# One group of eight PSUM banks in place of groups of three and five, in a hybrid state-space layer

## The chip, the cores and the metric

The kernel runs on one core of a Trainium2 chip. The metric is the device time of one execution in microseconds (us), as the median of several executions. Engines are named as in the profile: PE is TensorE's matrix products and PEld its weight loads, DVE is VectorE, ACT is ScalarE, POOL is GpSimd, SP is the engine whose queue issues the DMAs.

## What is computed

One layer of a sequence model over 512 latent tokens and a context of 256 tokens, width 1024. A normalised input goes through one wide projection; its columns feed three token mixers (an SSD scan with 16 heads, an mLSTM with 4 heads, a gated linear attention, GLA, with 4 heads), each run forwards and backwards. Each mixer's output is projected, the three are merged with gates, and one projection and a SwiGLU network follow. Cut to its joints:

```
h = concat(norm(ctx) * (1 + csc1) + csh1, norm(x) * (1 + sc1) + sh1)
parts = split(h @ w_in)
y_ssd, y_ml, y_gla = scans, both directions, of parts
merged = sum over the three of sigmoid(gate) * (y @ w_b)
x = x + g1 * (merged @ w_out)
x = x + g2 * ((silu(h2 @ w_g) * (h2 @ w_u)) @ w_ffn_out)
out = norm(x)
```

## The kernel before, in words

Activations lie channel by token: 128 channels on the partitions, 512 latent tokens (or 256 of the context) along the free dimension. Each fp32 weight is split into a high and a low part (`split` in `fetch`, lines 217 to 221: ACT makes the high part on line 218, DVE or POOL the low part on line 220), and a dense product of 1024 channels is 24 matmuls into one PSUM bank: eight slices of channels by three (high by high, high by low, low by high), line 321 in `dense`. A product with tokens on the partitions is `tok`, line 359. Weight pieces come by DMA into a ring of slots (line 226); a slot is free again once a dense product has read it.

PSUM has eight banks of 128 by 512 fp32. Before the change they are in two groups. `acc_bank` (line 176) gives a bank to dense products, from a group of three. `bank` (line 179) gives one to all other products: the transposes, the scans' small products, the row sums. It has a group of five. Each call makes a new tile; the tile takes a bank of its group that has been released, and the first matmul into it waits until the last reader of the bank's former tile is done. Banks are given to tiles when the program is built, not while it runs. I take it in what follows that a group hands out the bank that it has got back first.

Two things set the order of the work. PE's order is that of the Python code (line 1657, `manual_schedule` for PE alone). `jobs` (line 248) takes the dense products one by one from a queue, and after each one `advance` (line 301) moves every open scan on by a step, so PE runs a dense product, then a few scan products, then the next dense product, always in that order. The other engines' and the DMA queue's order is settled when the program is built, from what is ready there.

Places that the prediction speaks of:
- GLA's `decay` (line 1011): per direction a product of 512 (line 1024) and one of 256 (line 1028), each into a bank of its own, read by DVE on lines 1025 and 1029. They read `aup` and `sm`, which were made much earlier.
- GLA's scan: `pre` (line 1104) makes scaled queries and keys on POOL (lines 1112 to 1120), ACT (1121) and DVE (1122); `products` (line 1125) multiplies them on PE (line 1132), and ACT (line 1134, the first) or DVE (line 1136, the others) takes the result from its bank into `A`. `turn` transposes (line 1164), ACT reads (line 1165). `step` is lines 1170 and 1171. `head_turn` transposes on line 993 and ACT reads on line 996; POOL multiplies by the gate on line 1204.
- The mLSTM's `turn` transposes keys (line 864). The SSD scan's output is read from its bank by DVE on line 792.
- `gates` (line 450): ACT reads a bank on line 519.
- `prepare` (line 1267) splits the finished mixer outputs for the branch products: ACT on line 364, DVE on line 365.
- The feed-forward products (line 1828) use one bank of the first group and two of the second per block of 128 channels; ACT and DVE read them on lines 1839 to 1852.

Of the kernel before, what the change touches and what calls it, by code (L numbers as in the profile page):

```python
# [9 lines left out]
F32 = mybir.dt.float32  # L10
# [81 lines left out]
class Slots:  # L92


    def __init__(self, net, need):
        self.net, self.own, self.out = net, {}, {}
        self.more(need)
# [44 lines left out]
class Net:  # L142
    def __init__(self, ctx, tc, a, out, dump):
        self.ctx, self.tc, self.nc, self.a, self.out, self.dump = ctx, tc, tc.nc, a, out, dump
        nc = tc.nc
        self.V, self.S, self.G, self.T = nc.vector, nc.scalar, nc.gpsimd, nc.tensor
        self.dma = nc.sync.dma_start
        pool = lambda name, bufs=1, **kw: ctx.enter_context(tc.tile_pool(name=name, bufs=bufs, **kw))
        self.kp = pool("keep")
        self.wp = pool("w")  # L150
        self.pd = pool("pd", space=bass.MemoryType.PSUM)
        self.ps = pool("ps", space=bass.MemoryType.PSUM)
        self.dp = pool("dr", space=bass.MemoryType.DRAM)

# [19 lines left out]
            yield  # L174

    def acc_bank(self):
        return self.pd.tile([128, 512], F32, name="acc", bufs=3)

    def bank(self):
        return self.ps.tile([128, 512], F32, name="bank", bufs=5)  # L180

    def source(self, key):
        a = self.a
# [1831 lines left out]
```

## Time and profile before

| | us |
|---|---|
| Median of three runs | 1473.01 (1469.53 to 1474.08) |
| The profiled execution's own time | 1467.97 |
| Its span, first to last instruction | 1466.2 |
| PE busy | 1372.4 (94%) |
| DVE busy | 927.8 (63%) |
| ACT busy | 664.2 (45%) |
| POOL busy | 364.5 (25%) |

How to read it: a matmul's row starts when it starts, and what it waited for stands behind it in brackets as "[idle before <-the engine, tile and line whose end released it]". The granted clock (PEclk) is TensorE's clock as a share of 2.4 GHz; it has two levels here, 1.00 (2.4 GHz) and 0.50 (1.2 GHz). A wait for several things is put down to the one that came last.

### The profile page before, as it was taken

To read this page: it belongs to the slowest core of one execution; us is meant where nothing else is said; L and a number is where in the kernel's file an instruction comes from. 1 tells how busy PE (TensorE), PEld (TensorE's weight loads), DVE (VectorE), ACT (ScalarE), POOL (GpSimd) and SP (SyncE) were. 2 spreads that over 40 slices of the span, in tenths; PEclk is the share of its full clock that TensorE was granted. 3 is DMA by queue.
4 is the path that set the end of the run, shared out by engine and by line. 5 is a ranking of instruction groups with operands and counts; after the bars stand their busy time and mean duration, and the time that the engine had idled before them with its cause. 6 is when DMAs were issued, how large, how long until landed. Compare 5 with 4: busy or idle time off the path is not lost. (4 is left out here: it accounts for less than half of the span.)

```text
span 1466.2 us, 22065 instructions
## 1 busy us (share of the span) xinstructions
PE 1372.4 (94%) x8136; PEld 1185.8 (81%) x8136; DVE 927.8 (63%) x1664; ACT 664.2 (45%) x1247; POOL 364.5 (25%) x330
## 2 busy tenths in 40 slices
PE   6998999999989999998997878999998999999997
PEld 4787789887778886886886866888778999998886
DVE  4557644968585567677675766434438988887332
ACT  5545464552244443334362553243346656566231
POOL 2115434124222123212324443134444000000011
PEclk9999999999999999999999998999998999999999
DMA  9323222333453224255546356757431333324331
GB/s 373 138 65 122 91 72 87 84 104 101 117 143 98 83 95 135 72 137 141 171 149 205 119 191 213 235 176 239 153 108 51 116 111 97 111 87 126 95 93 61
DMA packets 98411, 189.31 MB, mean 129 GB/s; under 512 B 10672, under 2 KB 19376, under 8 KB 97152
## 3 DMA queue, kind: packets, MB, share of 16 engines
q1 hardware_dynamic: 98304, 187.91, 41.3%
q8 instruction: 64, 1.05, 0.3%
q14 instruction: 43, 0.35, 0.1%
HBM read 166.73 MB, written 20.61 MB: 128 GB/s over the span
## 5 line engine op out<-in xcount | busy, mean ns | idle before, releaser
L321 PE MATMUL acc<-hlh,w 128*128 128x512 f32 (+1 forms) x1160 | 385.1, 400 | 6.1 <-ACT w L218 2.5
L218 ACT CAST w<-w 128x512 fp32r<-128x512 f32 (+1 forms) x302 | 182.8, 613 | 366.1 <-DMA w<-in_w_main_dram 162.0
L220 POOL TENSOR_TENSOR w<-w,w 128x512 fp32r<-128x512 f32 x125 | 173.8, 1390 | 540.0 <-ACT w L218 492.9
L321 PEld LDWEIGHTS acc<-hlh,w 128*128 128x128 f32 x1160 | 221.5, 191 | 57.9 <-ACT w L218 3.0
L220 DVE TENSOR_TENSOR w<-w,w 128x512 fp32r<-128x512 f32 x177 | 136.5, 774 | 203.9 <-ACT w L218 169.3
L321 PE MATMUL acc<-hll,w 128*128 128x512 f32 (+1 forms) x576 | 226.9, 394 | 0.9 <-POOL hll L1563 0.9
L321 PEld LDWEIGHTS acc<-hll,w 128*128 128x128 f32 x576 | 110.2, 191 | 23.6 <-POOL hll L1563 1.1
L1785 ACT CAST w<-w 128x512 fp32r<-128x512 f32 x140 | 85.0, 623 | 33.8 <-PE bank L1828 25.5
L321 PE MATMUL acc<-t,w 128*128 128x512 f32 x360 | 89.1, 401 | 9.9 <-ACT t L364 9.3
L1786 DVE TENSOR_TENSOR w<-w,w 128x512 fp32r<-128x512 f32 x140 | 94.5, 685 | 5.0 <-ACT w L1785 4.6
L359 PE MATMUL acc<-w,hlh 128*128 128x256 f32 x512 | 96.3, 290 | 0.2 <-POOL w L220 0.2
L1828 PE MATMUL acc<-th,w 128*128 128x256 f32 x480 | 95.5, 281 | 0.2 <-ACT fm L1839 0.2
L321 PEld LDWEIGHTS acc<-t,w 128*128 128x128 f32 x360 | 68.0, 190 | 26.7 <-ACT t L364 9.7
L1544 POOL TENSOR_TENSOR sq<-sq,sq 128x512 f32<-128x512 f32 x6 | 7.8, 1300 | 307.9 <-ACT sq L1542 307.9
L359 PEld LDWEIGHTS acc<-w,hlh 128*128 128x128 f32 x512 | 81.5, 194 | 3.4 <-issue 1.8
L439 DVE SCALAR_TENSOR_TENSOR cacc<-acc,c_scanc,cacc 128x510 f32<-128x510 f32 (+3 forms) x124 | 77.5, 631 | 6.7 <-ACT cacc L435 5.9
L1828 PEld LDWEIGHTS acc<-th,w 128*128 128x128 f32 x480 | 77.8, 188 | 0.5 <-ACT fm L1839 0.4
L321 PE MATMUL acc<-row,w 128*128 128x512 f32 (+1 forms) x360 | 76.3, 365 | 1.2 <-ACT row L367 0.7
L359 PE MATMUL acc<-w,hll 128*128 128x256 f32 x256 | 73.4, 287 | 0.0
L321 PEld LDWEIGHTS acc<-row,w 128*128 128x128 f32 x360 | 61.3, 189 | 13.6 <-ACT row L367 1.1
L1828 PE MATMUL acc<-tl,w 128*128 128x256 f32 x240 | 67.3, 281 | 0.0
L321 PE MATMUL acc<-hx,w 128*128 128x256 f32 (+1 forms) x432 | 63.7, 302 | 0.0
(454 smaller groups left out, 2902.4 us busy)
## 6 DMA issues: line engine op xcount, KB each, us to landing
w<-in_w_main_dram SPq DMA_DIRECT2D x180, 256.0 KB, 3.4
w<-in_w_ffs_dram SPq DMA_DIRECT2D x80, 256.0 KB, 2.7
t<-in_wmodT_dram SPq DMA_DIRECT2D x32, 512.0 KB, 3.9
w<-in_w_b_dram SPq DMA_DIRECT2D x48, 256.0 KB, 4.0
xk<-gd SPq DMA_DIRECT2D x40, 256.0 KB, 3.6
w<-in_w_ffo_dram SPq DMA_DIRECT2D x40, 256.0 KB, 2.6
wmod<-in_wmod_dram SPq DMA_DIRECT2D x8, 1024.0 KB, 11.0
row<-rows SPq DMA_DIRECT2D x16, 512.0 KB, 6.0
```

The costliest lines, as they stand in the source:

```text
L218: self.S.copy(h, w)
L220: self.LE[self.wcount % len(self.LE)].tensor_sub(l, w, h.bitcast(F32))
L321: self.T.matmul(dst, w[:, m0:m1], x[:, c0:c1], start=(k == 0 and j == 0), stop=(k == nk - 1 and j == 2))
L359: self.T.matmul(p, x[:, t0:t0 + 128], w, start=(k == 0 and j == 0), stop=(k == KT - 1 and j == 2))
L439: V.scalar_tensor_tensor(acc[:, o0:o1], p[:, o0 + d:o1 + d], w[:, cc, j:j + 1], acc[:, o0:o1], op0=OP.mult, op1=OP.add)
L1544: self.G.tensor_add(a, a, t)
L1785: S.copy(H, x)
L1786: le[p % 7].tensor_sub(L, x, H.bitcast(F32))
L1828: T.matmul(dst, x, y, start=(first and k == 0 and j == 0), stop=(k == 3 and j == 2), skip_group_check=True)
```

## The change

Both helpers now make a tile of the same group, `bank`, which has eight banks. The group of three is gone. Nothing else is touched: the same instructions are issued with the same operands, and only the numbers of the banks differ, and with them what a first matmul waits for.

```diff
         self.kp = pool("keep")
         self.wp = pool("w")
-        self.pd = pool("pd", space=bass.MemoryType.PSUM)
         self.ps = pool("ps", space=bass.MemoryType.PSUM)
...
     def acc_bank(self):
-        return self.pd.tile([128, 512], F32, name="acc", bufs=3)
+        return self.bank()
 
     def bank(self):
-        return self.ps.tile([128, 512], F32, name="bank", bufs=5)
+        return self.ps.tile([128, 512], F32, name="bank", bufs=8)
```

## Rows read from the trace of the kernel before

**Rows 1.** The page: the span, and each engine's busy time.
```profile
span 1466.2 us, 22065 instructions
...
PE 1372.4 (94%) x8136; PEld 1185.8 (81%) x8136; DVE 927.8 (63%) x1664; ACT 664.2 (45%) x1247; POOL 364.5 (25%) x330
```

**Rows 2.** Waits of PE, whole run: releaser, us in total, times, longest us.
```profile
PE acc L321 <- ACT t L364: 9.3, 1, 9.3
...
PE bank L1132 <- ACT xk L1165: 6.4, 1, 6.4
PE bank L1028 <- ACT xk L1134: 5.0, 1, 5.0
PE bank L1170 <- DVE xk L1136: 4.6, 2, 3.7
...
PE bank L864 <- DVE xk L792: 4.1, 1, 4.1
PE bank L1132 <- ACT t L519: 3.7, 1, 3.7
...
PE bank L1024 <- DVE t L1025: 1.5, 1, 1.5
...
PE bank L1024 <- DVE xk L1136: 1.2, 1, 1.2
...
PE acc L1828 <- ACT fm L1839: 0.2, 1, 0.2
```

**Rows 3.** Windows: stretch, length, busy us of the engines, PEclk, DMA share, GB/s.
```profile
133.30:136.70 3.40, 3.40 (x14) 3.21 (x15) 3.40 (x12) 2.44 (x8) 1.34 (x3) 0.50 0.25 80
404.60:432.90 28.30, 23.65 (x147) 20.82 (x148) 27.55 (x70) 11.53 (x22) 7.67 (x6) 0.88 0.55 150
423.90:430.20 6.30, 5.92 (x27) 5.52 (x28) 5.65 (x20) 2.95 (x6) 0.68 (x2) 0.50 0.54 164
432.90:457.60 24.70, 24.26 (x187) 22.16 (x185) 10.51 (x34) 11.16 (x21) 2.70 (x3) 1.00 0.30 84
795.80:798.90 3.10, 3.10 (x13) 3.01 (x14) 3.10 (x6) 1.76 (x4) 0.59 (x1) 0.50 0.49 184
822.80:826.20 3.40, 3.40 (x17) 3.31 (x16) 2.44 (x5) 2.20 (x4) 2.23 (x3) 0.50 0.54 201
870.60:873.90 3.30, 3.28 (x13) 3.18 (x14) 3.10 (x5) 2.51 (x5) 3.06 (x3) 0.50 0.00 0
1135.00:1330.00 195.00, 194.81 (x1638) 194.51 (x1637) 170.96 (x318) 120.66 (x244) 0.00 (x0) 1.00 0.35 106
```

**Rows 4.** Timeline of PE, 788 to 799 us: start, length, line, operands.
```profile
788.80 1.05 PE L1132 MATMUL bank<-row 128*128 128x128 f32 x8
789.69 0.49 PE L1164 MATMUL bank<-c_ident,row 128*128 128x128 f32 x3
789.94 0.48 PE L1024 MATMUL bank<-sm,aup 128*128 128x512 f32 x1
790.25 0.28 PE L1028 MATMUL bank<-sm,aup 128*128 128x256 f32 x1
790.37 0.40 PE L1024 MATMUL bank<-sm,aup 128*128 128x512 f32 x1
795.77 0.58 PE L1028 MATMUL bank<-sm,aup 128*128 128x256 f32 x1 [5.00 <-ACT xk L1134]
...
798.51 0.64 PE L321 MATMUL acc<-hlh,w 128*128 128x512 f32 x1
```

**Rows 5.** Timeline of ACT around 795 us.
```profile
794.61 0.62 ACT L218 CAST w<-w 128x512 fp32r<-128x512 f32 x1 [4.96 <-DMA w<-in_w_main_dram]
795.14 0.58 ACT L1134 COPY xk<-bank 128x512 f32<-128x512 f32 x1
```

**Rows 6.** Timelines of PE, POOL and ACT, 870 to 886 us.
```profile
885.76 0.79 PE L321 MATMUL acc<-t,w 128*128 128x512 f32 x1 [9.29 <-ACT t L364]
...
871.24 1.97 POOL L1204 TENSOR_TENSOR xk<-xk,xk 128x512 f32<-128x512 f32 x1 [0.24 <-ACT xk L996]
...
885.10 0.60 ACT L364 CAST t<-xk 128x512 fp32r<-128x512 f32 x1
```

## The prediction

> **What bounds the kernel now.** I read the page first. PE is busy 1372.4 of 1466.2 us [rows 1]: the kernel is bound by PE's row of products, run in a fixed order. A change that adds and removes no product can only alter the 93.8 us in which PE stands idle (1466.2 less 1372.4) and the stretches in which its clock is down.
>
> So the next view is the list of PE's waits [rows 2], read with one question: which of these waits is for data, and which for a bank? A wait is for a bank when the releaser reads a PSUM tile that the waiting product has no use for. Line 1028 multiplies `sm` by `aup`; its releaser, line 1134, copies a GLA product out of its bank. Nothing ties the two but the bank. Line 864 transposes mLSTM keys, and line 792 reads the SSD scan's output from its bank. By the same test lines 1165, 1136, 1025 and 519 are readers of other tiles' banks. Seven rows are of this kind: 6.4 + 5.0 + 4.6 + 4.1 + 3.7 + 1.5 + 1.2 = 26.5 us. Every one has `bank` as its tile, so each is a wait in the group of five. The largest wait of a dense product, 9.3 us behind line 364, is for data. For the group of three the list has a single row, 0.2 us behind line 1839. The banks that are short are those of the scans, while the dense products' three cost nothing.
>
> The third view is the granted clock behind these waits [rows 3]. After five of them it reads 0.50, the 1.2 GHz level: PE works 3.40 + 5.92 + 3.10 + 3.40 + 3.28 = 19.1 us there, and at 2.4 GHz that work would take half. The waits thus cost another 9.6 us, 36.1 us in all. That is the ceiling of what the change can give.
>
> **The change, part by part.** It issues no instruction more or less: matmuls, reads and DMAs are the same, on every queue. Its cost in work is nothing, and needs no cover. What it changes is when a product may start.
>
> Before, a scan product waits once five tiles of its group are unread, whatever the other three banks do. After, it waits only once eight tiles of any kind are unread. Eight unread tiles before the change would mean that both groups are full, when either kind of product would wait as well. If banks are handed out in the order in which they come back, the change therefore adds no wait of its own; it only takes some away. What remains to be worked out is how much of each wait goes and what is late next. With the clock's share, the five large places are:
>
> - 133 us, line 519's bank: 3.7 of wait and 3.40/2 = 1.7 of clock, 5.4 us.
> - 424 us, line 792's bank: 4.1 and 5.92/2 = 3.0, 7.1 us. Here DVE is the late one: it is busy 27.55 of 28.30 us up to 432.9 [rows 3], so PE gets ahead of it. But behind that it is busy 10.51 of 24.70 us only, waiting for others, and can catch up.
> - 795 us, line 1134's bank: five tiles are unread when PE comes to line 1028 again, namely lines 1132, 1164, 1024, 1028 and 1024 [rows 4]. ACT, which must read the first, has stood 4.96 us behind a weight cast that waited for its DMA [rows 5]. In one group of eight, line 1028, the next product and the next transpose take the sixth, seventh and eighth bank; the dense product after them would be the ninth, and stands until the first of the five is read at 795.7 us. It starts at 798.51 now. So 798.5 less 795.8, 2.7 us, is gained of 5.0 + 1.55: a dense product waits there for a scan's bank, which it never did before.
> - 822 us, line 1136's bank: 3.7 and 3.40/2, 5.4 us.
> - 870 us, line 1165's bank: 6.4 and 3.28/2 = 1.6, 8.0 us. I count nothing for it. The next thing PE needs is the split of line 364, which ACT ends at 885.7; PE stands 9.29 us for it already [rows 6]. ACT gets there behind a chain of POOL's work that begins after POOL's line 1204 at 871.24, itself released by ACT and not by PE. Earlier products at 864 would only make PE's wait at 885 longer.
>
> The small ones, 4.6 less 3.7 of line 1170, 1.2 and 1.5 of line 1024, are 3.6 us. Without the last place the sum is 5.4 + 7.1 + 2.7 + 5.4 + 3.6 = 24.2 us.
>
> Not all of that arrives at the end, since PE meets late data sooner. Places from 735 us on (1.5 + 2.7 + 5.4 = 9.6) all run into the wait at 885; ACT, POOL and the DMA queue come earlier to it only as far as they were held up by PE, and I keep a third, 3.2 us. Of the other 14.6 I keep two thirds, 9.7 us, since DVE, the busiest of the readers, has a third of its time free [rows 1] and mostly moves with PE. Bounds are none and all. Sum: 12.9, say **13 us**. From 900 us on there is next to nothing to gain: the only bank wait there is the one of 0.2 us.
>
> One cost has no row. PE's order is fixed, but the other queues' order is settled at building, and with other banks it may come out otherwise. The nearest row is ACT's 4.96 us behind one weight cast [rows 5]: one such meeting more or one fewer is 5 us either way. I take 0 and keep both ends.
>
> A rule speaks against the change. At full clock PE runs through the feed-forward products of 1135 to 1330 us, three banks to a block from both groups in turn, without a drop [rows 3]. The Trainium skill, TensorE: Matmul & The Clock Gate, "A second HAM failure mode: psum-queue depth-cycling", tells of a kernel whose turning through PSUM banks left small gaps between products, with the clock swinging between its levels. By it, eight banks in turn would bring more half-speed stretches; the trace speaks against that for this kernel.
>
> **The sum against the times.** The profiled execution took 1467.97 us, 5.0 below the median of 1473.01. 1468 less 13 is 1455; on the scale of the median, 1473 less 13 is **1460 us**.
>
> **Rivals.**
>
> *The waits only move (20%).* All that PE gains up to 870 us may be given back at 885, where it waits for the last mixer's output; and the DVE-bound stretch up to 432.9 may pass its lateness on to 457. For it: PE's 9.3 us is the largest wait after the start and lies right behind the bank waits. Against it: the chain to 885 begins with products that PE itself would deliver sooner. The time would be that of before, 1473, within 4 us. The same TensorE page, "HAM oscillation — how this bites in real kernels", reports a kernel in which double-buffered PSUM gave no further gain once its order of loops was right (126.6 against 125.5 us).
>
> *Slower (13%).* A dense product's bank may be one whose reader is late. Since banks are tied to tiles at building, a dense product may be given the bank of a scan tile that the builder thought read and that the chip reads late; before, a dense product could not meet one. The place is the GLA scans, four heads; the price is one wait like 5.0 or 6.4 us per head [rows 2], some 20 us with the gains above gone: up to 1493. It decides once two of four heads meet such a bank. Against it: the order of return must differ by three banks or more, as eight are in turn.
>
> *All of it (7%).* Every wait goes and the data come earlier with PE: 1473 less 36 is 1437.
>
> **How the numbers follow.** A measurement of this kernel tells a difference from none at about 0.3%, 4.4 us. My forecast, a gain between 5 and 28 us, has 60%. Faster by more than 0.3% is 60 + 7, 67%; within 0.3% 20%; slower 13%. The likeliest time is 1460. The range starts at 1473 less 28.1 (36.1 without the last place), 1445, and reaches past no change to 1475; below it lies the 7%, above it most of the 13%. The 5 us of the queues' order lie inside.
>
> **What would show it.** In PE's waits the rows behind 1134, 792, 519 and 1136 are gone or under 1 us, and the clock near 133, 424 and 822 us stays at 1.00; PE's busy time falls by the clock's share and its idle by more. Near 795 a dense product waits for line 1134. The wait of line 321 behind 364 grows from 9.3 towards 15 us. I am wrong if line 321 or 359 waits for lines 1134, 1136 or 1165 in several heads, or if the data waits grow by as much as the bank waits shrink.

## The result and the profile after

| | before | after |
|---|---|---|
| Median of runs on one chip, us | 1471.76 (1469.53 to 1474.08, 4 runs) | 1451.19 (1447.94 to 1455.69, 4 runs) |
| The profiled execution's own time, us | 1467.97 | 1447.94 |

The ratio of the times is 0.988 (95% interval 0.9855 to 0.9905): **faster**, by 20.6 us; a small gain, 1.2%, but clear of the scatter. The same pair, run again twice below, gave 17.8 and 17.3 us. The forecast was 13 us faster, 1460 us, with a range of 1445 to 1475. The sign and the range held; the gain is a third to six tenths larger than the forecast. The lines of the kernel after are one lower than before from line 151 on, so line 320 is what line 321 was, and every PSUM tile is now called `bank`.

The page of the kernel after, against [rows 1]:

```profile
span 1446.2 us, 22042 instructions
...
PE 1364.4 (94%) x8136; PEld 1178.1 (81%) x8136; DVE 926.3 (64%) x1664; ACT 661.9 (46%) x1247; POOL 367.8 (25%) x330
```

PE has the same 8136 products, and the other engines' counts are the same too. The 23 instructions by which the total is lower are semaphore instructions (27 fewer at PE, 1 fewer at SP, 5 more at DVE), so the prediction's "no instruction more or less" holds for the work alone. PE's busy time fell by 8.0 us (1372.4 to 1364.4) and its idle time by 12.0 (93.8 to 1446.2 less 1364.4, 81.8); together that is the 20.0 us of the span. So in this pair of executions the gain came from the two sources that the prediction named, waits and clock, in the ratio 3 to 2; the prediction's ceiling had them as 26.5 to 9.6. The ratio is that of one pair. In the profiles of the two repeats below the idle time is 83.4 and 78.7 us and the busy time 1377.4 and 1374.8: there all of the gain is idle time. Over all executions of those two series the mean granted clock is 0.9738 before and 0.9775 after in the first (13 and 4 executions), 0.9722 and 0.9774 in the second (11 and 5). An estimate from these shares and the spans gives the clock 6 of 17.8 us and 8 of 17.3.

PE's waits after, against [rows 2]. The columns are the waiting product, its releaser, us in total, times, longest.

```profile
PE bank L378 <- DVE sq L1445: 12.4, 1, 12.4
PE bank L320 <- ACT t L363: 10.6, 1, 10.6
...
PE bank L320 <- ACT xk L1133: 4.3, 1, 4.3
...
PE bank L320 <- ACT xk L1164: 3.3, 1, 3.3
...
PE bank L1236 <- DVE xk L1135: 2.5, 1, 2.5
PE bank L614 <- ACT t L597: 2.4, 1, 2.4
...
PE bank L358 <- ACT row L1070: 1.6, 1, 1.6
...
PE bank L948 <- DVE dn L952: 1.3, 1, 1.3
...
PE bank L646 <- DVE xk L1135: 1.0, 1, 1.0
...
PE bank L320 <- ACT ctanh L1256: 0.7, 1, 0.7
...
PE bank L1131 <- DVE xk L1135: 0.4, 1, 0.4
...
PE bank L948 <- ACT ctanh L968: 0.3, 1, 0.3
```

Read them with the prediction's question, data or bank. Of the seven bank rows of before, those behind lines 519, 792 and 1025 are gone. What is left behind the readers 1133, 1164 and 1135 is 4.3 + 3.3 + 1.0 + 0.4 = 9.0 us of the 26.5. By the same test four rows are new: lines 358, 948 (twice) and 320 wait for lines 1070, 952, 968 and 1256, which read banks that these products have no use for, 1.6 + 1.3 + 0.3 + 0.7 = 3.9 us. That makes 12.9 us of bank waits, against 27.5 before (the prediction's seven rows leave out 0.6 us of line 1028 behind line 1025 and 0.4 of line 868 behind line 958). The 2.5 us of line 1236 is another kind: that product multiplies the `A` which line 1135 writes, so it waits for data. The wait behind line 363 (line 364 before) grew by 1.3 us only, from 9.3 to 10.6.

The granted clock in the five stretches of [rows 3], found again in the kernel after by the same PE instructions. The columns are the stretch, its length, busy us of PE, PEld, DVE, ACT and POOL, the clock, DMA share and GB/s. The last row is 200 us of the feed-forward products.

```profile
126.60:130.00 3.40, 2.67 (x19) 2.25 (x17) 1.35 (x4) 1.11 (x2) 1.70 (x2) 1.00 0.39 120
412.90:419.20 6.30, 6.30 (x52) 6.03 (x51) 5.82 (x19) 2.87 (x7) 1.30 (x1) 1.00 0.90 221
781.10:784.20 3.10, 3.07 (x7) 2.48 (x8) 3.10 (x6) 3.10 (x5) 3.10 (x4) 0.50 0.81 297
803.00:806.40 3.40, 3.40 (x28) 3.32 (x27) 3.40 (x7) 0.50 (x2) 3.40 (x5) 1.00 0.03 10
854.20:857.50 3.30, 3.20 (x8) 2.52 (x9) 3.12 (x5) 2.59 (x6) 3.06 (x3) 0.50 0.00 0
1120.00:1320.00 200.00, 199.90 (x1647) 197.96 (x1646) 176.33 (x328) 126.60 (x255) 0.00 (x0) 1.00 0.35 105
```

Three of the five run at 2.4 GHz now, those where the wait is gone. Two still run at 1.2 GHz, behind the two largest bank waits that are left. Both hold in the two repeats too. In the long stretch the clock stays at 1.00 with eight banks in turn. The swinging clock that the Trainium skill tells of (TensorE: Matmul & The Clock Gate, "A second HAM failure mode: psum-queue depth-cycling"), which the prediction weighed against the change, did not come there; nor did small gaps, as PE is busy 199.90 of 200.00 us.

**Where along the run the gain arises.** PE runs the same products in the same order in both kernels, so the start of the n-th one can be subtracted. The table gives how much earlier (us) a product starts than in the profiled execution of before, for three executions of the kernel after and for two experiments told below.

| start in before | what lies there | after | again, 1st | again, 2nd | keys only | last head only |
|---|---|---|---|---|---|---|
| 129.07 | ahead of the wait at 133 | 2.7 | 2.6 | 2.5 | 0.9 | 0.6 |
| 133.22 | behind it | 6.6 | 6.4 | 6.4 | 1.0 | 0.7 |
| 404.75 | ahead of 424 | 6.5 | 6.0 | 9.0 | 2.0 | 1.2 |
| 430.10 | behind 424 and its slow stretch | 13.8 | 11.2 | 15.2 | 9.3 | 0.8 |
| 733.13 | ahead of the 1.5 us wait of line 1024 | 16.1 | 11.8 | 16.4 | 11.7 | 3.7 |
| 735.32 | behind it, ahead of the last mixers' scans | 18.0 | 13.6 | 18.2 | 10.5 | 0.1 |
| 827.08 | behind 795 and 822 | 20.9 | 16.4 | 21.2 | 12.0 | -1.2 |
| 862.06 | ahead of the wait at 870 | 14.4 | 9.8 | 14.2 | 10.7 | -1.3 |
| 870.62 | behind the wait at 870 | 21.0 | 16.3 | 20.7 | 10.1 | 2.0 |
| 872.99 | the next dense product | 18.7 | 12.4 | 19.7 | 10.1 | 0.2 |
| 885.76 | behind the wait for line 364 | 16.3 | 10.1 | 17.3 | 9.3 | -1.9 |
| 1400.12 | feed-forward | 20.0 | 5.3 | 13.0 | 12.5 | -0.8 |

Up to 735 us the gain builds up and, with small steps back, stays. From there to 885 it goes up and down, between 21.0 and 14.4 us in the first execution, because the waits that are left stand at other places than those of before; at 885.76 the three executions are within 2 us of where they were at 733.13. The last line differs by 15 us between three executions of one kernel: that is mostly the clock, of which more at the end.

### The profile page after: what moved, and what is told of

The parts are those of the page before. It is cut to its first block, busy times and chain, and to the rows that moved or that the text cites. A ratio compares the mean times of both kernels' runs of the same rounds, so it can differ in the third digit from the quotient of the medians.

```text
span 1446.2 us, 22042 instructions
## 1 busy us (share of the span) xinstructions
PE 1364.4 (94%) x8136; PEld 1178.1 (81%) x8136; DVE 926.3 (64%) x1664; ACT 661.9 (46%) x1247; POOL 367.8 (25%) x330
## 5 line engine op out<-in xcount | busy, mean ns | idle before, releaser
L320 PE MATMUL bank<-hlh,w 128*128 128x512 f32 (+1 forms) x1312 | 422.3, 395 | 9.1 <-ACT xk L1133 4.3
L320 PEld LDWEIGHTS bank<-hlh,w 128*128 128x128 f32 x1312 | 245.8, 190 | 67.3 <-ACT xk L1133 4.6
L320 PE MATMUL bank<-hll,w 128*128 128x512 f32 (+1 forms) x648 | 252.1, 389 | 0.9 <-POOL hll L1562 0.9
L320 PEld LDWEIGHTS bank<-hll,w 128*128 128x128 f32 x648 | 123.5, 191 | 25.5 <-POOL hll L1562 1.1
L1827 PE MATMUL bank<-th,w 128*128 128x256 f32 x640 | 124.7, 282 | 0.1
L320 PE MATMUL bank<-t,w 128*128 128x512 f32 x360 | 90.2, 405 | 14.6 <-ACT t L363 10.6
L1827 PEld LDWEIGHTS bank<-th,w 128*128 128x128 f32 x640 | 103.1, 189 | 0.5 <-ACT fm L1838 0.5
L358 PE MATMUL bank<-w,hlh 128*128 128x256 f32 x512 | 94.7, 287 | 0.7 <-POOL w L219 0.7
L1827 PE MATMUL bank<-tl,w 128*128 128x256 f32 x320 | 90.1, 282 | 0.0
L1827 PE MATMUL bank<-hlh,w 128*128 128x256 f32 x400 | 82.2, 284 | 4.2 <-DVE w L1785 4.2
```

The costliest lines, as they stand in the source:

```text
L320: self.T.matmul(dst, w[:, m0:m1], x[:, c0:c1], start=(k == 0 and j == 0), stop=(k == nk - 1 and j == 2))
L358: self.T.matmul(p, x[:, t0:t0 + 128], w, start=(k == 0 and j == 0), stop=(k == KT - 1 and j == 2))
L1827: T.matmul(dst, x, y, start=(first and k == 0 and j == 0), stop=(k == 3 and j == 2), skip_group_check=True)
```

## The experiments

My theory: eight banks in one group take away waits that came from the split into 3 and 5, and what is won before 735 us arrives, while what is won from there to 885 us is lost again. The rivals: the number of the scans' banks does it, not the sharing; the dense products' third bank was idle; or the new order of the other queues does it.

**Other splits: two and six, four and four.** Both keep two groups.

```diff
-        return self.pd.tile([128, 512], F32, name="acc", bufs=3)
+        return self.pd.tile([128, 512], F32, name="acc", bufs=2)
-        return self.ps.tile([128, 512], F32, name="bank", bufs=5)
+        return self.ps.tile([128, 512], F32, name="bank", bufs=6)
-        groups, done, banks = [], [], [3]
+        groups, done, banks = [], [], [2]
```

> Dense products keep two banks, the scans get six; nothing is shared (the startup's first products take two banks of the dense group and one of the other). If a short scan group is the whole cause, the scans' bank waits (26.5 us before) fall by half or more and the time by 8 to 16 us, to 1456 to 1464. If the dense products' third bank is in use too, though the list of waits shows next to nothing for it, dense products now wait for the readers of the convolutions (DVE line 439, which end up to 10 us after the product): 1475 to 1510.

Measured: 1484.74 us against 1469.5, ratio 1.0107 (1.0065 to 1.0148), slower. PE's waits with two and six:

```profile
PE acc L321 <- DVE cacc L439: 14.0, 7, 4.0
...
PE acc L359 <- ACT xc L1063: 6.8, 2, 5.7
PE bank L1132 <- ACT xk L1134: 6.8, 1, 6.8
```

The last changed line concerns the startup alone: how many of its first products take a bank of the dense group. The dense products now stand 14.0 us in seven places for line 439, the convolution on DVE that reads their banks, and some 24 us for banks in all. The scans' bank waits, with six banks, come to 19.4 us: a quarter less than 26.5, and not the half or more that was expected. In [rows 2] their group has a row of 0.2 us, from which the prediction read that their three banks cost nothing. That held; but a list of waits tells only that three are enough, not that two would be.

The other split has `bufs=4` in both groups and `banks=[4]`.

> Dense products four banks, scans four, nothing shared. If the scans' banks are the short ones: more scan products wait than in the kernel before, bank waits of 45 to 80 us in place of 26.5, and the time is 1485 to 1515. If the gain of the shared group came from the other queues' changed order and not from banks: within 5 us of 1472, with no order by size among the splittings.

Measured: 1479.59 us, ratio 1.0064 (1.0034 to 1.0094). Slower, though by less than was expected. The scans' bank waits come to some 36 us, where 45 to 80 were expected. The rows of before are there and mostly longer (6.9 behind line 1134, 6.8 behind 1165, 4.7 behind 519, 4.3 behind 792, 4.5 behind 1136), and new ones beside them, the largest 4.2 behind line 953.

**One group of seven.** The kernel after with one bank fewer.

```diff
-        return self.ps.tile([128, 512], F32, name="bank", bufs=8)
+        return self.ps.tile([128, 512], F32, name="bank", bufs=7)
```

> One group of seven banks, the eighth left unused. If it is the sharing that pays: most of the gain stays, 1450 to 1460, with the wait of the dense product behind the late reader near 781 us some us longer. If it is the number of banks that a scan stage can have (eight instead of five): about half is gone, 1460 to 1470.

Measured: 1456.72 us, ratio 0.9909 (0.9878 to 0.994). Seven shared banks beat eight that are split 3 and 5, 2 and 6, or 4 and 4. **It is the sharing that pays**; the eighth bank adds what lies between 0.9909 and the 0.988 of the kernel after, and their intervals overlap. Seven in one group also let a scan stage have more than five at a time; the test parts sharing from the eighth bank, and not from that. The sum of the bank waits doesn't show it: it is some 22 us here, little less than the 27.5 before. In the profiled execution idle time is 88.0 us and busy time 1366.9, 5.8 and 5.5 less than before, so about half of its gain there is the clock.

**One place alone.** In the kernel before, the two transposes of the mLSTM's `turn` (lines 862 and 866) take a bank of the dense group; all else stays. This is to take away the wait of line 864 at 424 us alone.

```diff
-            b = self.bank()
+            b = self.acc_bank()
...
-            b = self.bank()
+            b = self.acc_bank()
```

> As before, groups of three and five, but the mLSTM's two key transposes take their banks from the dense group. That takes away the one wait near 424 us behind line 792 and little else. By the prediction's term for this place: 7.1 us of which two thirds arrive, so 4 to 7 us faster, 1465 to 1468, and the clock stays up there. If the wait only moves on to the next late data: within 2 us of 1472.

Measured: 1457.32 us, ratio 0.9923 (0.9894 to 0.9952), 11 us faster with 7 to 16 inside the interval. PE's waits of this kernel, where line 864 has no row any more and the others of [rows 2] stand, some of them longer:

```profile
PE bank L1132 <- ACT xk L1165: 7.1, 1, 7.1
PE bank L1028 <- ACT xk L1134: 7.0, 1, 7.0
...
PE bank L1132 <- ACT t L519: 3.6, 1, 3.6
PE bank L1170 <- DVE xk L1136: 3.6, 2, 2.8
```

The table's column shows where it comes from: 2.0 us ahead of the place, 9.3 behind it, so 7.2 there (7.1 was worked out for wait and clock together), and 11.7 at 733 us. Nothing of the place's gain is given back up to there, where I had written it off in part. The measured gain is larger than the place's own 7.2 us. The rest lies elsewhere: 2.0 us ahead of the place, 2.5 from there to 733 us, and 2.6 near 1100 us (from 9.8 early at 1090 to 12.4 at 1110), where the profile of before has a slow stretch. These runs don't tell whether that is scatter of the clock or the new order of the other queues.

**The wait at 870 us alone.** In the kernel before, the last GLA head's `products` takes its banks from the dense group.

```diff
-            b = self.bank()
+            b = self.acc_bank() if self.scans == 4 and self.lasth == h else self.bank()
```

> As before, groups of three and five, but the products of the last GLA scan (line 1132 of the fourth head) take their banks from the dense group. That takes away the wait of 6.4 us near 870 us. By the prediction nothing of it arrives: the wait of line 321 behind line 364 grows from 9.3 to 14 to 16 us, and the time stays within 3 us of the kernel before. If bank waits are worth what they last: 6 to 8 us faster.

Measured: 1473.17 us, ratio 1.0002 (0.9979 to 1.0025): no difference. The removal was not a clean one:

```profile
PE acc L321 <- ACT t L364: 10.2, 1, 10.2
...
PE acc L1132 <- DVE xk L1219: 3.1, 1, 3.1
...
PE acc L321 <- DVE xk L1219: 2.2, 1, 2.2
```

The 6.4 us behind line 1165 became 3.1 and 2.2 us for dense banks. PE is 1.3 us late at 862.06 and 2.0 us early at 870.62, so 3.3 us were won. But the 2.2 us wait takes them back at once: at 872.99 PE is 0.2 us early. The wait behind line 364 was to grow to 14 to 16 us and grew to 10.2, and PE is 1.9 us late behind it. So this kernel does not put the forecast for this place to the test; what does is the stretch that ends the wait, measured below.

**The kernel after, again.**

> The changed kernel once more, beside the next three on one chip: 0.985 to 0.991 of the kernel before, 1450 to 1458 us.

Measured: 1453.82 us against 1471.6, ratio 0.9874 (0.9836 to 0.9913).

> The changed kernel for the third time, beside the next three on one chip: 0.984 to 0.992 of the kernel before.

Measured: 1455.24 us against 1472.54, ratio 0.9885 (0.9864 to 0.9907). Three comparisons give 0.9874 to 0.9885.

**The wait at 781 us, where a dense product stands for line 1133.** DVE takes the copy instead of ACT, which is late behind a weight cast:

```diff
-                S.copy(A, i4(b))
+                V.tensor_copy(A, i4(b))
```

> The changed kernel, with the first product of each GLA scan copied out of its bank by DVE instead of ACT. In the changed kernel a dense product waits 4.3 us near 781 us for that copy, which stands behind a weight cast on ACT, and the clock is at 1.2 GHz for 6.8 us there. If the copy's place behind the cast is the cause: that wait is gone and the time 3 to 7 us below the changed kernel's, 1445 to 1450. If DVE is held up as well there, or what is gained at 781 is lost again at 869: no difference within 3 us.

Measured: 1456.32 us, ratio 0.9883 (0.9855 to 0.9911): no difference from the kernel after. The trace says why. PE and ACT around the place in this kernel:

```profile
783.52 0.80 PE L320 MATMUL bank<-hlh,w 128*128 128x512 f32 x1 [4.32 <-ACT row L1164]
...
782.47 0.62 ACT L217 CAST w<-w 128x512 fp32r<-128x512 f32 x1 [4.56 <-DMA w<-in_w_main_dram]
783.00 0.47 ACT L1164 COPY row<-bank 128x384 f32<-128x384 f32 x1
```

The next reader on ACT, line 1164, stands behind the same weight cast, so the product waits 4.3 us for its bank in place of the first one's. To move one reader away from the late queue only shows the next one there.

**The wait behind line 363.** Four runs of three kernels, all from the kernel after. The first kernel takes one block of gate products (two dense products) from the second `F2` of the plan and gives it to the last `F`:

```diff
-PLAN = "g0 g1 b s0 F2 F2 m0 m1 s1 m2 m3 M g2 g3 F5 B0 B1 B2"
+PLAN = "g0 g1 b s0 F2 F1 m0 m1 s1 m2 m3 M g2 g3 F6 B0 B1 B2"
```

> The changed kernel, with one block of gate products (two dense products, about 11 us of TensorE) taken out of the early part of the order and put among the last ones. In the changed kernel TensorE stands 10.6 us near 869 us for the last mixer's output, the largest wait after the start, and the clock is at 1.2 GHz for 13.7 us around it. If the chain of the last scan sets that point, work moved there is free: 8 to 15 us below the changed kernel, 1436 to 1444. If the early scans lose their cover by as much: no difference, or slower by up to 5 us.

> The kernel with one block of gate products moved late, once more. If its first reading (0.983 against 0.987 for the changed kernel) was a difference: 3 to 8 us below the changed kernel again. If it was scatter: within 3 us of it.

Measured: 1450.2 us, 0.9834 (0.9807 to 0.9861), and the second time 1453.55, 0.9873 (0.9851 to 0.9895). The wait is still 10.9 us in the first. Its time did not come back, so this is no better version.

The second takes work off POOL's chain ahead of the wait: the products by the gate (line 1203), two of which stand there, go to DVE. The third has both edits.

```diff
-            G.tensor_mul(yw[m], yw[m], tg[m])
+            V.tensor_mul(yw[m], yw[m], tg[m])
```

> The changed kernel, with the multiplication by the gate at the end of each GLA scan (line 1203, 1.3 to 2.0 us on POOL) done by DVE. Two of these stand ahead of the last scan's chain on POOL, and the stores behind them hold up the loads on SP's queue. If that chain sets the wait of 10.6 us near 869 us: the wait shrinks by 2 to 5 us and the time by as much. If the wait is set by ACT's own order, in which the split stands behind the scan's exponentials whatever POOL does: no difference within 2 us.

> Both edits on the changed kernel. If they help apart and don't meet: the sum of the two, 5 to 13 us below the changed kernel, 1440 to 1450 us. If both work on the same wait: no better than the better one.

Measured: 1454.5 us, 0.9876 (0.9849 to 0.9904), and with both edits 1452.71, 0.9872 (0.9849 to 0.9894). The wait is 9.0 us in the first of them. None of the three is told apart from the kernel after; no version found here beats it.

The traces of these kernels show what sets this wait. In the kernel after, PE, ACT, POOL and one row of DVE; the columns are start, length, engine, line, operands, and in brackets the idle time before and its releaser:

```profile
854.30 4.52 PE L320 MATMUL bank<-t,w 128*128 128x512 f32 x12 [3.26 <-ACT xk L1164]
869.43 0.79 PE L320 MATMUL bank<-t,w 128*128 128x512 f32 x1 [10.61 <-ACT t L363]
...
852.66 0.62 ACT L217 CAST w<-w 128x512 fp32r<-128x512 f32 x1 [2.16 <-DVE w L219]
853.18 0.59 ACT L1217 ACTIVATE xk<-bank 128x512 f32<-128x512 f32 x1
853.67 0.58 ACT L1164 COPY xk<-bank 128x512 f32<-128x512 f32 x1
854.14 1.28 ACT L995 ACTIVATE xk<-bank,c_scanc 128x512 f32<-128x512 f32 x2
...
867.81 1.06 ACT L1120 ACTIVATE row<-row 128x1024 f32<-128x1024 f32 x1 [1.99 <-POOL row L1119]
868.77 0.60 ACT L363 CAST t<-xk 128x512 fp32r<-128x512 f32 x1
...
854.92 1.99 POOL L1203 TENSOR_TENSOR xk<-xk,xk 128x512 f32<-128x512 f32 x1 [0.24 <-ACT xk L995]
...
862.06 1.23 DVE L1121 TENSOR_TENSOR row<-row,row 128x1024 f32<-128x1024 f32 x1 [3.96 <-ACT row L1120]
...
862.10 1.67 POOL L1118 TENSOR_TENSOR hx<-t 128x256 f32<-128x256 f32 x1
863.74 0.63 POOL L1119 TENSOR_TENSOR hx<-t 128x256 f32<-128x256 f32 x1
```

The cast that PE waits for stands on ACT behind line 1120, which waits for POOL. POOL works without a gap from 854.92 to 867.77 us, two products by the gate and twelve subtractions of another head's `pre`. From the start of line 995 on ACT to that cast it is 868.77 less 854.14, 14.63 us. In the kernel before it is 885.10 [rows 6] less 870.46, 14.64 us:

```profile
870.46 1.28 ACT L996 ACTIVATE xk<-bank,c_scanc 128x512 f32<-128x512 f32 x2
```

**The stretch has the same length to 0.01 us**, whatever PE has won; in the two repeats it is 14.59 and 14.63 us, in the kernel with the last head alone 14.65. And its start is not given by PE at this place. It comes 16.3 us earlier than in the kernel before (870.46 less 854.14), while PE's products just ahead of it come 14.4 us earlier (862.06 in the table): ACT comes to line 995 behind weight casts, one of which waits 2.16 us for DVE, while PE's transposes for it (line 992) start at 847.56 us. What was not tried is ACT's order, which puts the cast behind line 1120: the loads of the cast's own data (line 1294) start at 859.63 us and take 3.6 us by the median, so by that estimate the first cast's data is there some 5 us before the cast. How much of the wait another order would save is open, since POOL's chain runs to 867.77 and a weight load, issued at 862.55 with 6.0 us to landing, to about 868.6.

With the gate's products on DVE the same stretch is 867.86 less 853.86, 14.00 us, and 14.00 again with both edits: 3.26 us of work taken from POOL gave 0.63. ACT, POOL and DVE of that kernel:

```profile
853.86 1.28 ACT L995 ACTIVATE xk<-bank,c_scanc 128x512 f32<-128x512 f32 x2
...
867.86 0.60 ACT L363 CAST t<-xk 128x512 fp32r<-128x512 f32 x1
...
854.36 1.63 POOL L1111 TENSOR_TENSOR row<-t 128x256 f32<-128x256 f32 x1
...
858.02 0.61 POOL L1119 TENSOR_TENSOR row<-t 128x256 f32<-128x256 f32 x1
...
865.27 1.60 POOL L1119 TENSOR_TENSOR row<-t 128x256 f32<-128x256 f32 x1
...
854.13 1.36 DVE L1397 SCALAR_TENSOR_TENSOR xk<-t 128x1024 bf16<-128x1024 f32 x1
...
864.74 1.65 DVE L1397 SCALAR_TENSOR_TENSOR xk<-t 128x1024 bf16<-128x1024 f32 x1
```

The twelve subtractions took 12.94 us in place of 10.08, because more of them lie beside work on DVE: 2.86 of the 3.26 us came back that way.

## Why the prediction was right, and where its size was off

- *PE bounds, and the gain can come from its waits and its clock alone*: right. Idle -12.0 and busy -8.0 make up the span's -20.0; in the repeats' profiles they are -10.4 and +5.0, and -15.1 and +2.4.
- *Rows 2 read as bank waits*: right, with 1.0 us left out. One group takes away 17.5 of the 26.5 us behind these readers and brings 3.9 behind others; the experiment on line 864 shows for one of them that only the bank tied it.
- *Eight shared banks add no wait of their own; 795 us in particular*: right for the place, not shown for the rest. Dense products wait 4.3 + 3.3 + 1.6 + 0.7 = 9.9 us for banks in the kernel after and 0.2 before. Since PE comes to these places 7 to 20 us earlier, that doesn't contradict the argument, but no run bears it out either. At 795 a dense product became the ninth tile and stands 4.33 us for line 1133, as forecast:

```profile
775.07 0.40 PE L1023 MATMUL bank<-sm,aup 128*128 128x512 f32 x1
775.30 0.28 PE L1027 MATMUL bank<-sm,aup 128*128 128x256 f32 x1
775.42 1.05 PE L1131 MATMUL bank<-row 128*128 128x128 f32 x8
776.31 0.49 PE L1163 MATMUL bank<-c_ident,row 128*128 128x128 f32 x3
781.13 0.79 PE L320 MATMUL bank<-hlh,w 128*128 128x512 f32 x1 [4.33 <-ACT xk L1133]
```

Against [rows 4] the second line starts 20.5 us earlier, the first one 15.3 and the dense product 17.4: 2.1 us stay where 2.7 were worked out.
- *424 us, 7.1 us; 133 us, 5.4 us*: the sizes hold to 2 us. The first gave 7.2, 5.3 and 6.2 us in three executions, and 7.2 alone. At 133 the wait's 3.8 us came, and 0.7 to 0.9 us of the clock's 1.7 by the product at 137 us.
- *870 us, counted 0*: right, and for the reason given. PE is 21.0 us early behind that wait and 16.3 behind the one for line 363; in between a dense product stands 3.3 us for line 1164's bank. The stretch of 14.6 us on ACT and POOL is the same in both kernels, and its end is what PE waits for in either.
- ***"Of the other 14.6 I keep two thirds, 9.7 us"***: **this is the term that was mis-sized.** At 733.13 us, just ahead of the places from 735 us on, the kernel after is 16.1, 11.8 and 16.4 us early. The places counted gave 4.6, 4.6 and 4.7 us at 133 with the clock, 7.2, 5.3 and 6.2 at 424, and -0.8, -1.2 and +1.7 between the two, where the small ones stood with 2.1. That is 11.0, 8.7 and 12.7 of the 14.6, a little over 9.7 on the mean. What is missing went near the places themselves: new bank waits behind line 1135 (0.4 and 1.0 us), and line 614's wait for data at 174 us, which takes 0.8 to 2.4. The reason given for the discount, that late readers farther on take a part back, is not seen: from 430 to 733 us PE gains another 2.4, 0.5 and 1.1 us, and 2.5 in the experiment on one place. The larger part of the error is what the sum had at nothing, without a reason: that gain, and 2.5 to 2.7 us ahead of 133 us, where the 0.6 us row of line 1028 that was left out is gone and the slow stretch of before at 20.6 us did not come.
- *"I keep a third, 3.2 us" of the places from 735 on*: too much. From 733.13 to 885.76 us the three executions change by +0.2, -1.7 and +1.0 us. A third was a guess between none and all; none is what the stretch of equal length gives. On the way new waits take back what the old ones gave: lines 948, 358 and 320 for banks, line 1236 for data (2.5 us).
- The two errors have opposite signs, which is luck: 9.7 + 3.2 = 12.9 was forecast up to 885 us, and 16.3, 10.1 and 17.3 were found there.
- *Nothing from 900 us on*: no bank wait is there in either kernel but the 0.2 us of before, yet PE's start moves by +3.7, -4.8 and -4.4 us between 885 and 1400 us in the three executions. In the first it is the slow stretch near 1099 us that did not come. The three medians (17.3 to 20.6 us) lie above the 16.3 of the profiles also because the profiled execution of before is 3.8 us faster than its median.
- *The queues' order, 5 us either way, taken as 0*: left open. DVE has at least 22 of its instructions in another place, ACT 19, POOL 2, SP 1. The kernel with line 864's place alone moves at least 7 instructions on DVE and 4 on ACT, none on the others. 7.2 us of its gain arise at the place itself, where the bank wait went, so that part is not a matter of order; for the whole change no kernel holds the orders and changes the banks.
- *Rivals.* That the waits only move is right for the places after 735 and wrong before. That a dense product meets a late scan bank happened at 781 us (4.3) and 854 us (3.3), twice, as often as I said would decide. It did not, since these stand where scan products waited 5.0 and 6.4 us before [rows 2], and the gains ahead of them stayed.
- *Signs named*: near 133, 424 and 822 us the clock stays at 1.00, and the rows behind 519 and 792 are gone, as named. Of those behind 1134 and 1136, 4.3 and 1.4 us are left, at other products. PE's busy time fell in one of three profiles only. The wait behind 364 was to grow towards 15 us and grew to 10.6; 3.3 us more stand just ahead of it, for line 1164's bank. PE arrives earlier there, but so does the stretch that ends the wait, by 16.3 us, about what PE had won by 733 us (10.0 and 17.3 us in the repeats).

## What to carry to other kernels

A buffer group per use looks tidy, but a wait in one group while the other has buffers free is the price; share one group when the users' peaks fall at different times, and test a split of another size before you call the smaller group idle. Tell a wait for a bank from a wait for data before you size it, and look among the waits of the new kernel for new ones of the same kind; their sum before is not the gain. Discount a gain by where it lies: in this kernel, what PE won after the last mixers' scans had begun was lost where PE waits for a chain that it does not hold up, and what it won earlier reached the end of that chain too. To find that chain, measure it in the trace from its first instruction to the one waited for, and ask who released the first.

## What the runs showed of the hardware that was not expected

**A POOL subtraction's time depends on what DVE does.** The same 128x256 subtraction takes 0.62 to 0.66 us with DVE idle and 1.6 us or a little more when it starts beside a 128x1024 operation of DVE: in the kernel after, line 1118 at 862.10 takes 1.67 us, and DVE runs line 1121 from 862.06 to 863.29; the next, at 863.74 with DVE idle, takes 0.63. The Trainium skill, Perfetto Trace Analysis, "Optimizing Scalar/DVE Operations", says that the two engines share a read port, so that moving operations between them might not help. These runs agree: 3.26 us moved to DVE, 2.86 of them back in longer subtractions. A subtraction that is under way when DVE starts is not lengthened: with the gate on DVE, line 1112 at 859.66 takes 0.65 us, though DVE's line 1121 starts at 859.76.

**The clock scatters between executions of one kernel.** PE's busy time is 1364.4 us in the profile of the kernel after and 1377.4 in the first repeat, for the same 8136 products, and the granted clock is 0.983 and 0.974. The times are 1447.94 and 1462.65 us. So 13 of the 14.6 us between two spans (1460.8 less 1446.2) are products at the lower clock. It is not a matter of the chip alone: the kernel with the gate on DVE took 1445.04 us at 0.984 and 1456.27 at 0.975 in the same series. A single profile of a changed kernel can therefore not size a gain of this kind; the median of several runs can, and the gains of the three pairs here differ by 3.3 us.
